# RMS norm and swish over 16384 rows: the first four stores are held back until the eleventh unit

## The chip, the cores and the metric

The kernel runs on one core of a Trainium2 chip. The metric is the device time of one execution in microseconds. Beside it there is a profiled execution, whose records give a span (from the first recorded instruction to the last), the busy time of each engine, the waits, and the packets of the DMA engines.

## The reference

The input `x` has 16 x 1024 = 16384 rows of 512 fp32 numbers. Each row is normalised and passed through swish:

```
rms = np.sqrt(np.mean(x ** 2, axis=-1, keepdims=True) + eps)
x_norm = x / rms * gamma
return (x_norm * (1.0 / (1.0 + np.exp(-x_norm)))).astype(np.float32)
```

That is 33.55 MB to read and 33.55 MB to write.

## The kernel before

**Tiles.** The 16384 rows are 128 rows for each of the 128 partitions. They are cut into eleven tiles (`sizes`, line 30) of 4, 4, 8, six times 16, 8 and 8 rows per partition. A partition's rows of one tile lie next to each other in DRAM, so a tile of n rows is moved as 128 runs of 2n KB: 8 KB for 4 rows, 16 KB for 8, 32 KB for 16.

**The ring.** One SBUF buffer, `xb`, has room for 96 rows per partition (`ring`, line 31). A row stays in its place from the load to the store: normalisation and swish are done in place. Tiles 0 to 7 are the first 96 rows and fill the ring. Tile 8 goes to the place of tiles 0, 1 and 2, and tiles 9 and 10 go to the place of tile 3. So load 8 must wait until stores 0, 1 and 2 have landed, and loads 9 and 10 until store 3 has (lines 112 to 122).

**Loads.** All loads are issued by SyncE (SP), in the order of the tiles, on its own DMA queue (q1 in the profile). The first two are placed ahead of the start-up code. Loads 0 to 7 have no wait and are issued in the first microseconds.

**Units.** Compute goes in units of four rows per partition (`cn`, line 33), so there are K = 32 units, and a tile has one, two or four of them. Unit k goes through these steps:

- `square(k)` on ScalarE (ACT): row 3 is squared and summed by one activation (line 165), rows 0 to 2 are squared into PSUM by another (line 172). The first unit of a tile waits for the tile's load.
- `sums(k)` on VectorE (DVE): a reduction of the three squared rows (line 213).
- on GpSimd (POOL): eps is added (line 147) and the power -1/2 is taken (line 154), on four numbers per partition.
- `norm(k)` on VectorE: four instructions, one for each row, that multiply by the row's factor and by gamma (line 224).
- `swish(k)` on ScalarE: one activation over the four rows (line 184).

PSUM has two buffers for the squares, so `square(k)` waits for `sums(k - 2)`. VectorE's order is sums(0), sums(1), norm(0), sums(2), norm(1), and so on.

**Stores.** Stores are issued by ScalarE on its own DMA queue (q10), in between its activations, and each waits for the swish of its tile's last unit (line 189). Their place in ScalarE's order is set by the loop at lines 201 to 208: at step k it puts down square(k), then each store whose tile ended at unit k - 2 or earlier (`ends` counts the units up to a tile's end: 1, 2, 4, 8, 12, 16, 20, 24, 28, 30, 32), then swish(k - 2). Store 0 thus comes at k = 3, store 1 at k = 4, store 2 at k = 6, store 3 at k = 10, store 4 at k = 14, and later ones at 18, 22, 26, 30, 32 and 34. At the end SyncE waits for every store that it hasn't waited for already.

Of the kernel before, what the change touches and what calls it, by code (L numbers as in the profile page):

```python
# [9 lines left out]
def kernel(  # L10
# [21 lines left out]
    early = 2  # L32
    cn = 4
    n_sq = 3
    N = sum(sizes)
    assert N * P == R, (N, R)

# [7 lines left out]
    T = len(tiles)  # L45
# [7 lines left out]
    ends = []  # L53
# [107 lines left out]
    def square(k):  # L161
        t, at, first = chunks[k]
        if first:
            nc.scalar.wait_ge(ld[t], 16)
        acc = nc.scalar.activation(  # L165
            out=junk[k % 2], in_=xb[:, at + n_sq, :], func=AF.Square,
            scale=inv_d**0.5, accum_out=ms[:, k, n_sq : n_sq + 1],
        )
        if k >= 2:
            need(acc, s_acc, k - 1)  # L170
        acc.then_inc(s_acc, 1)
        square = nc.scalar.activation(  # L172
            out=sq[k % 2][:, 0:n_sq, :], in_=xb[:, at : at + n_sq, :],
            func=AF.Square, scale=inv_d**0.5,
        )
        if k >= 2:
            need(square, s_sum, k - 1)
        square.then_inc(s_sq, 1)

    def swish(k):  # L180
        _, at, _ = chunks[k]
        rows = xb[:, at : at + cn, :]
        need(
            nc.scalar.activation(out=rows, in_=rows, func=AF.Silu), s_norm, k + 1  # L184
        ).then_inc(s_swish, 1)

    def store(t):
        need(
            nc.scalar.dma_start(out=dram(of, t), in_=buf(t)), s_swish, ends[t]
        ).then_inc(st[t], 16)  # L190
# [9 lines left out]
    stored = 0  # L200
    for k in range(K + 3):
        if k < K:
            square(k)
        while stored < T and ends[stored] <= k - 2:
            store(stored)
            stored += 1
        if 2 <= k < K + 2:
            swish(k - 2)
# [74 lines left out]
```

## Time and profile before

| | us |
|---|---|
| median of 4 runs | 160.23 (159.94 to 160.59) |
| the profiled execution, its own time | 160.33 |
| its span | 159.0 |
| VectorE busy | 139.0 (87%) |
| ScalarE busy | 125.3 (79%) |
| GpSimd busy | 91.7 (58%) |
| moved by the DMA engines | 67.15 MB, 422 GB/s on average |

In a row of a table of transfers, the share of a queue is the time that its packets took, as a part of the time of all 16 DMA engines. A row of waits reads: the engine and line that waited, whom it waited for, microseconds in total, how often, and the longest. In a timeline a row gives the start and the duration in microseconds, the engine, the line and the operation, and in brackets the idle time ahead of it and who ended it. A DMA issue is counted from the instruction's start, its landing is the moment when the last of the 16 engines reports completion.

The last four loads, and eight of the eleven stores, were issued and landed at these times (us):

| tile | rows per partition | load issued | landed |
|---|---|---|---|
| 7 | 16 | 4.4 | 81.8 |
| 8 | 16 | 62.0 | 101.2 |
| 9 | 8 | 81.3 | 115.7 |
| 10 | 8 | 81.7 | 130.2 |

| tile | store issued | landed after |
|---|---|---|
| 0 | 18.1 | 16.3 |
| 1 | 22.5 | 24.1 |
| 2 | 31.1 | 30.8 |
| 3 | 48.3 | 33.0 |
| 4 | 65.6 | 35.0 |
| 8 | 134.6 | 14.6 |
| 9 | 143.3 | 10.9 |
| 10 | 151.6 | 7.4 |

### The profile page before, as it was taken

Reading aid. Unit: us, or ns where it says so; the run is one execution under the profiler, and the core shown is the slowest. Engines: PE = TensorE matmul, PEld = TensorE weight load, DVE = VectorE, ACT = ScalarE, POOL = GpSimd, SP = SyncE. Lnnn points to the kernel's source line nnn. Section 1 sums busy time; section 2 is a strip of 40 time slices with the busy share of each in tenths; the row PEclk is TensorE's granted clock in tenths of the full one; section 3 lists DMA queues with packets and bytes.
Section 4 is the critical chain, followed back from the end, with each engine's and each line's share of the span. In section 5 each row is a group of like instructions: output and inputs, shape, how many; then the busy total and the mean of one; then the engine's idle time right before and its main releaser. Section 6 shows DMA issues by size and latency. Waiting matters only on the chain.

```text
span 159.0 us, 439 instructions
## 1 busy us (share of the span) xinstructions
DVE 139.0 (87%) x162; ACT 125.3 (79%) x129; POOL 91.7 (58%) x71
## 2 busy tenths in 40 slices
DVE  0239999999999999999999999999999999996600
ACT  0835989888888888998888888888998888883410
POOL 2035444444455555544488889888888888889000
DMA  6999999899999999999999999999999999999996
GB/s 247 422 505 412 396 433 460 371 480 418 414 398 511 396 414 441 412 429 478 412 398 478 429 412 404 429 470 425 412 437 433 412 486 412 396 495 412 400 420 284
DMA packets 3323, 67.15 MB, mean 422 GB/s; under 512 B 500, under 2 KB 500, under 8 KB 504
## 3 DMA queue, kind: packets, MB, share of 16 engines
q1 hardware_dynamic: 1584, 33.56, 49.6%
q10 hardware_dynamic: 1736, 33.57, 49.2%
q14 instruction: 3, 0.02, 0.0%
HBM read 33.56 MB, written 33.56 MB: 422 GB/s over the span
## 4 chain that ended last, share of the span: by engine, by line
DVE 84%; DMA 5%; POOL 3%; ACT 1%; issue 1%; POOLq 0%
DVE xb L224 52%; DVE ms L213 32%; DMA gamma<-in_gamma_dram 5%; POOL aeps L147 2%; ACT xb L184 1%; POOL rstd L154 1%; DVE gamma_sb L237 0%; POOL gamma L142 0%; POOL blank L141 0%; POOLq L65 0%
## 5 line engine op out<-in xcount | busy, mean ns | idle before, releaser
L224 DVE SCALAR_TENSOR_TENSOR xb<-xb,rstd,gamma_sb 128x512 f32<-128x512 f32 x128 | 87.9, 762 | 1.2 <-POOL rstd L154 1.2
L147 POOL TENSOR_SCALAR aeps<-ms 128x4 f32<-128x4 f32 x32 | 52.4, 1639 | 50.8 <-DVE ms L213 50.8
L184 ACT ACTIVATE xb<-xb 128x2048 f32<-128x2048 f32 x32 | 61.1, 1909 | 19.2 <-DVE xb L224 19.2
L213 DVE TENSOR_REDUCE ms<-sq 128x3 f32<-128x1536 f32 x32 | 56.5, 1767 | 7.0 <-ACT sq L172 7.0
L172 ACT ACTIVATE sq<-xb 128x1536 f32<-128x1536 f32 x32 | 45.9, 1434 | 0.0
L154 POOL TENSOR_TENSOR rstd<-aeps,neg_half 128x4 f32<-128x4 f32 x32 | 38.4, 1201 | 2.7
L165 ACT ACTIVATE junk<-xb 128x512 bf16<-128x512 f32 x32 | 19.7, 615 | 3.4 <-DMA xb<-in_x_dram 3.4
L165 ACT ACTIVATION_READ_ACCUMULATOR junk<-xb 128x1 f32 x32 | 6.0, 186 | 0.0
L199 ACT ACT_TABLE_LOAD x1 | 1.3, 1283 | 3.6 <-issue 3.6
L237 DVE LOAD_MASK_SELECT gamma_sb<-gamma x1 | 0.0, 14 | 2.4 <-DMA gamma<-in_gamma_dram 2.4
L141 POOL MEMSET blank<- 128x16 f32 x1 | 0.1, 111 | 1.5 <-POOLq L65 1.5
L237 DVE STREAM_SHUFFLE gamma_sb<-gamma 128x512 f32<-128x512 f32 x1 | 0.7, 718 | 0.0
L142 POOL MEMSET gamma<- 128x512 f32 x1 | 0.5, 524 | 0.0
L264 POOL MEMSET const-float32-0.0<- 128x1 f32 x1 | 0.1, 98 | 0.2 <-issue 0.2
L264 POOL MEMSET const-bfloat16-1.0<- 128x1 bf16 x1 | 0.1, 101 | 0.0
L264 POOL MEMSET const-uint8-127<- 128x1 uint8 x1 | 0.1, 101 | 0.0
L143 POOL MEMSET neg_half<- 128x4 f32 x1 | 0.1, 101 | 0.0
L264 POOL MEMSET const-float32-1.0<- 128x1 f32 x1 | 0.1, 98 | 0.0
## 6 DMA issues: line engine op xcount, KB each, us to landing
xb<-in_x_dram SPq DMA_DIRECT2D x6, 4096.0 KB, 41.6
out_dram<-xb ACTq DMA_DIRECT2D x6, 4096.0 KB, 31.2
xb<-in_x_dram SPq DMA_DIRECT2D x3, 2048.0 KB, 34.3
out_dram<-xb ACTq DMA_DIRECT2D x3, 2048.0 KB, 10.9
xb<-in_x_dram SPq DMA_DIRECT2D x2, 1024.0 KB, 5.9
out_dram<-xb ACTq DMA_DIRECT2D x2, 1024.0 KB, 20.2
scratch<-blank ACTq DMA_DIRECT2D x1, 8.0 KB, 7.8
gamma<-in_gamma_dram ACTq DMA_DIRECT2D x1, 8.0 KB
```

Source lines behind the costliest of these rows:

```text
L141: nc.gpsimd.memset(blank, 0.0).then_inc(s_blank, 1)
L142: nc.gpsimd.memset(gamma4, 0.0).then_inc(s_zero, 1)
L147: nc.gpsimd.tensor_scalar(out=aeps[:, k, :], in0=ms[:, k, :], scalar1=eps_f, scalar2=None, op0=ALU.add,),
L154: nc.gpsimd.tensor_tensor(out=rstd[:, k, :], in0=aeps[:, k, :], in1=neg_half, op=ALU.pow),
L165: acc = nc.scalar.activation(out=junk[k % 2], in_=xb[:, at + n_sq, :], func=AF.Square, scale=inv_d**0.5, accum_out=ms[:, k, n_sq : n_sq + 1],)
L172: square = nc.scalar.activation(out=sq[k % 2][:, 0:n_sq, :], in_=xb[:, at : at + n_sq, :], func=AF.Square, scale=inv_d**0.5,)
L184: nc.scalar.activation(out=rows, in_=rows, func=AF.Silu), s_norm, k + 1
L199: nc.scalar.preload_act_table_set("silu_and_others")
L213: nc.vector.tensor_reduce(out=ms[:, k, 0:n_sq], in_=sq[k % 2][:, 0:n_sq, :], op=ALU.add, axis=mybir.AxisListType.X,),
L224: ins = nc.vector.scalar_tensor_tensor(out=row, in0=row, scalar=rstd[:, k, j : j + 1], in1=gamma_sb, op0=ALU.mult, op1=ALU.mult,)
L237: nc.vector.stream_shuffle(gamma_sb, gamma4, [0] * 32), s_gld, 16
L264: nc = _bacc.Bacc("TRN2", target_bir_lowering=False, num_devices=1)
```

## The change

A number `held` is set to 11, and the loop that puts down stores does so only from step 11 on. At k = 11 stores 0, 1, 2 and 3 are due together and are put down one after the other, between square(11) and swish(9). Stores 4 to 10 are due at step 14 and later and keep their places. Nothing else is changed.

```diff
@@ -32,6 +32,7 @@
     early = 2
     cn = 4
     n_sq = 3
+    held = 11
     N = sum(sizes)
     assert N * P == R, (N, R)
 
@@ -201,7 +202,7 @@
     for k in range(K + 3):
         if k < K:
             square(k)
-        while stored < T and ends[stored] <= k - 2:
+        while k >= held and stored < T and ends[stored] <= k - 2:
             store(stored)
             stored += 1
         if 2 <= k < K + 2:
```

## The prediction

> **What bounds the kernel now.** I read the page's totals and slices first, then who waited for whom, then the chain that ended last, then the transfers by stretch, and last the stretch around the moved stores. The page (busy time by engine, busy tenths in 40 slices, transfer queues with packets, MB and share of 16 engines):
>
> ```profile
> span 159.0 us, 439 instructions
> DVE 139.0 (87%) x162; ACT 125.3 (79%) x129; POOL 91.7 (58%) x71
> ...
> DMA  6999999899999999999999999999999999999996
> ...
> q1 hardware_dynamic: 1584, 33.56, 49.6%
> q10 hardware_dynamic: 1736, 33.57, 49.2%
> ```
>
> The DMA engines are full from the first slice to the last. q1 has the loads, q10 the stores; together their packets take 98.8% of 159.0, or 157.1 us, and only 1.9 us is not packet time. At the same time VectorE (DVE) is at 9 in nearly every slice. What VectorE waits for, and then three pieces of the chain of waits (start, length):
>
> ```profile
> DVE ms L213 <- ACT sq L172: 7.0, 1, 7.0
> DVE gamma_sb L237 <- DMA gamma<-in_gamma_dram: 2.4, 1, 2.4
> DVE xb L224 <- POOL rstd L154: 1.2, 1, 1.2
> ```
>
> ```profile
> 52.35 2.65 DVE xb L224 x4
> 54.99 1.67 DVE ms L213
> ...
> 149.63 1.91 ACT xb L184
> ```
>
> VectorE waits three times in the whole execution: at the start for the first squares (7.0) and gamma (2.4), and at the end for GpSimd (1.2). Between, it repeats 2.65 + 1.67 = 4.32 us per unit. Its last row is done at 149.6, the last swish at 151.5, and the last store is issued at 151.57 and lands 7.4 us later, at 159.0. So two limits meet at the same end: the VectorE chain plus the last store, and the bytes. The store line's answer (issue ns min/median/max, first and last start, then issue to landing):
>
> ```profile
> L189 ACTq DMA_DIRECT2D out_dram<-xb x11: 338/339/339, 18.1 to 151.6; - x11
> ...
> DMA to landing us min/median/max: 7.4/24.1/35.0
> ```
>
> How close the two are: from 151.5 on the queues move 2.65 MB, of which the last store is 2.10, so 0.55 MB (1.3 us at 431 GB/s) was queued ahead of it. The engines hardly ran dry before the last store reached them.
>
> How the two queues share the engines, in 20 to 50 us and in 64 to 80 us:
>
> ```profile
> q1 hardware_dynamic: 366, 10.42, 81.8%
> q10 hardware_dynamic: 321, 2.64, 20.7%
> ```
>
> ```profile
> q10 hardware_dynamic: 114, 3.64, 52.8%
> q1 hardware_dynamic: 101, 3.24, 46.9%
> ```
>
> In the first stretch the loads are runs of 32 KB per partition and the stores mostly 8 and 16 KB, and the loads get four fifths; in the second both are 32 KB and they share evenly. The total is one (shares over 100% are packets cut by the stretch's ends).
>
> **What the Trainium skill says.** "DMA: Bandwidth & Descriptors", section "Queues, rings and completion order": an engine alternates between the queues at packet granularity. The shares just shown agree if a packet is one partition's run. The same page, "Issuing engines are not separate DMA queues": transfers from different issuers run on the same 16 engines and interleave; the trace agrees (one queue gives way to the other, the sum stays). Its section "Where 436 GB/s comes from" gives a ceiling of 435.2 GB/s, an estimate of 154.3 us for 67.15 MB at best; the trace has 157.1 us of packets. "Perfetto Trace Analysis", section "DMA Instruction — HWDGE (DVE, Sync)": the reported issue time ends when the sequencer is free for its next instruction. So the issue rows are what a burst costs ScalarE's queue.
>
> **The change part by part.** Units are numbered k. Stores 0 to 3 (4, 4, 8, 16 rows) are now issued at k = 11; before at k = 3, 4, 6, 10 (18.1, 22.5, 31.1, 48.3 us). Stores 4 to 10 are due at k = 14 and later and keep their places. No instruction is added or removed.
>
> *Where k = 11 falls.* Timeline around it:
>
> ```profile
> 52.53 0.61 ACT L165 ACTIVATE junk<-xb 128x512 bf16<-128x512 f32 x1
> ...
> 53.14 1.43 ACT L172 ACTIVATE sq<-xb 128x1536 f32<-128x1536 f32 x1
> ...
> 55.03 1.91 ACT L184 ACTIVATE xb<-xb 128x2048 f32<-128x2048 f32 x1 [0.45 <-DVE xb L224]
> ...
> 59.22 1.76 DVE L213 TENSOR_REDUCE ms<-sq 128x3 f32<-128x1536 f32 x1
> ```
>
> The first two lines are square(11). Store 3 went out at 48.34, 0.13 after square(10) began at 48.21, while that was executing; so here the first of four is issued at 52.66. Their waits are met: they need swish(7), finished before 48.3.
>
> *ScalarE's queue.* Behind the four stand swish(9), which begins at 55.03 because it waits for VectorE, then square(12), then the sum of unit 12 on VectorE at 59.22. Four issues at the 0.34 of the store row take 1.36 us and end at 54.0, hidden by square(11), which runs to 54.57, and by the 0.45 of waiting. The trace of before has no burst of stores. Its nearest rows are pairs: loads 9 and 10 on SyncE (SP) took 0.33 and 1.06, scratch and gamma on ScalarE 0.35 and 1.09, while six loads in a row took 0.33 to 0.56 each. Lower bound 1.36 us; upper 4 x 1.09 = 4.36. I take 0.34 + 3 x 0.5 = 1.8, ending at 54.5: cost nothing. Without this cover each microsecond would pass to swish(9); square(12) ends at 58.88 today, 0.34 ahead of its reader, and VectorE never catches up what it loses.
>
> *SyncE's queue.* Load 8 (rows 96 to 111) waits for stores 0 to 2, loads 9 and 10 for store 3. In bytes at 0.431 MB/us:
> - To 52.7 us the queues moved 21.90 MB in before; now all of it is loads, of 25.17 MB for 96 rows. 3.27 MB are left. With 1.5 us for a store's first bytes (the first load took 1.0), they meet stores at 54.2 with 2.6 MB to go; at four to one that is 3.3 MB, 7.7 us: load 7 is in at about 62, against 81.8 before (issued 4.39, 77.4 to landing).
> - Stores 0 to 2 are 4.19 MB, of which 0.66 have gone; 3.53 MB alone take 8.2 us: landed at about 71.5 (before 61.9). Load 8 is issued at 71.6, 9.6 us later than today, first bytes at 73.
> - By then 1.2 MB of store 3 are gone. The other 3.0 share evenly with load 8: 14 us, landed at 88.5 (before 81.3), when loads 9 and 10 are issued. Load 8 has 1.2 MB left, shared with store 4 (issued 65.6): in at 94 (before 101.2). Loads 9 and 10 (16 KB runs against 32 KB stores, one third) take 2.1 x 3 / 0.431 = 14.6 us each: in at about 108.5 and 123 (before 115.7 and 130.2).
> - Needed, at 4.316 us a unit from square(11) at 52.53: load 8 at square(24), 108.6; load 9 at square(28), 125.9; load 10 at square(30), 134.5. Margins of 14, 17 and 11 us, against 7, 10 and 4 before. Cost nothing.
>
> *Does an engine run dry?* To 62 there are loads. After that store 3 and store 4 (10 us each alone) follow without a gap. When the last load ends near 122, 51.8 MB have moved, 18.2 of it stores; 25.2 MB have been issued by 117.4. The 7 MB left last 16 us, to 138, and store 8 is issued at 134.6. From there queue and dates are those of before, since the same bytes have moved.
>
> *One queue alone.* Loads are alone for about 36 us more, stores for about 20 more. In 5 to 15 us the load queue alone shows 438 GB/s (101.9%), in 144 to 151 the store queue alone 440 (102.3%), against 436 and 431 shared. Stretches this short are uncertain by a packet at each end, some per cent. I take no difference and keep 1% either way: 55 us x 1% = 0.55 us.
>
> *Sum.* VectorE 0, burst 0, late loads 0, queues 0 to 0.1: span 159.1. The profiled execution was 160.33, 1.33 around its span, and 0.10 over the median of 160.23. So 159.1 + 1.33 - 0.10 = 160.3 us.
>
> **Rivals.**
> *The burst stalls VectorE (slower).* Place: swish(9) behind the four issues. If the last three cost 1.06 each, they end at 52.66 + 3.52 = 56.18, 1.15 late; less 0.34 of slack VectorE loses 0.81. At 4.36 us it loses 1.65. It decides from a burst of 2.71 us (52.66 to 55.37), and up to 1.3 us can vanish in the bytes queued ahead of the last store. Unhidden: 161.0, at worst 161.9. For it: two pairs with 1.06 and 1.09. Against: six loads in a row without one.
> *A queue alone leaves gaps (slower).* At 1%: 160.8. For: nothing alternates to cover a hand-over. Against: the slices of 9 before the first store.
> *Unmixed transfers are quicker, or GpSimd's last wait shrinks (faster).* The bytes could end up to 1.3 us earlier before the last store is late for its own sake: 158.9 at best; 1% gives 159.7. The 1.2 us that VectorE waits for GpSimd at the end, if gone, leaves the bytes where they are. Against: packets fill 157.1 of 159.0.
> *The change does only part of what it says.* 3.27 of the 25.17 MB still load beside stores; this moves no end: 160.3.
>
> **How the numbers follow.** About 0.3% (0.5 us) is what a measurement can tell from no change. The forecast has 0.78; the burst 0.08, gaps 0.07, a late load or dry queue that I missed 0.02; quicker transfers 0.05. So slower 0.17, same 0.78, faster 0.05. The forecast's own spread is 159.9 to 160.7 from the runs of before (159.94 to 160.59); widened to the 1% cases and to the unhidden 0.81 us: 159.7 to 161.0.
>
> **What would show it.** Right: VectorE still at 2.65 and 1.67 with three waits; four store issues between 52.6 and 55, with swish(9) at 55.0; SyncE waiting for stores to about 71.5 and 88.5; q10 empty before 54; the last store issued near 151.6. Wrong: a wait of VectorE for L172 or L165 in mid-run, ScalarE waiting for a load after 100 us, or slices under 9 in the DMA row near 54, 62 or 72 us.

## The result: 0.45% slower, and the profile after

The changed kernel took 160.93 us in the median of 39 runs (160.35 to 162.13), the kernel before 160.16 us in 60 runs beside it. The ratio is 1.0045, 95% interval 1.0032 to 1.0058: slower by some 0.7 us. A later series of six runs (`r1` below) gave 1.0078 (1.0059 to 1.0098); the two intervals don't meet, so two series of one kernel can differ by 0.3%, and smaller differences between ratios of different series can't be read. Ratios leave out executions more than 1.5% above the fastest of the same kernel, which in `r7` are 5 of 22 (165.56 to 167.58 us). The forecast was 160.3 us and no change. The time lies in the range given, but the likeliest case was not the one that came.

The profiled execution of the changed kernel took 160.93 us, with a span of 159.6. Its page, as before (busy time, busy tenths in 40 slices, queues with packets, MB and share of 16 engines):

```profile
span 159.6 us, 439 instructions
DVE 138.8 (87%) x162; ACT 125.2 (78%) x129; POOL 65.4 (41%) x71
...
DMA  7999999999999899999999999999999999999995
...
q1 hardware_dynamic: 1584, 33.56, 49.8%
q10 hardware_dynamic: 1736, 33.57, 49.0%
```

Same packets, same bytes, and still no idle stretch to speak of. But a share is a share of the span, so each is multiplied by it: the stores' packets (q10) took 0.490 x 159.6 = 78.2 us of 16 engines, as before (0.492 x 159.0 = 78.2); the loads' packets (q1) took 0.498 x 159.6 = 79.5 us against 0.496 x 159.0 = 78.9. The span grew by 0.6 us, and so did the time of the load packets. (A share is printed to a tenth of a per cent, 0.16 us; the packet records below are finer.)

What VectorE waits for, and the two ScalarE activations and the burst around k = 11 (timeline: start, length):

```profile
DVE ms L214 <- ACT sq L173: 7.0, 1, 7.0
DVE gamma_sb L238 <- DMA gamma<-in_gamma_dram: 2.2, 1, 2.2
```

```profile
50.51 1.91 ACT L185 ACTIVATE xb<-xb 128x2048 f32<-128x2048 f32 x1 [0.45 <-DVE xb L225]
50.52 1.83 ACTq L190 DMA_DIRECT2D out_dram<-xb  x4
...
54.83 1.91 ACT L185 ACTIVATE xb<-xb 128x2048 f32<-128x2048 f32 x1 [0.45 <-DVE xb L225]
```

The burst of four took 1.83 us and cost ScalarE nothing: swish(9) at 54.83 still waits the same 0.45 us for VectorE. VectorE has no wait in mid-run, and the wait for GpSimd at the end is gone, so the last store is issued early:

```profile
L190 ACTq DMA_DIRECT2D out_dram<-xb x11: 338/339/488, 50.5 to 150.0; - x11
...
DMA to landing us min/median/max: 9.5/20.7/38.9
```

At 150.0 instead of 151.6, and yet it lands at 159.6 instead of 159.0: 9.5 us after its issue instead of 7.4. Compute is done sooner and the bytes later. The waits of SyncE for stores came out as worked out (load 8 issued at 72.2, loads 9 and 10 at 87.9; forecast 71.6 and 88.5):

```profile
SPq L121 <- DMA out_dram<-xb: 67.2, 1, 67.2
SPq L123 <- DMA out_dram<-xb: 15.4, 1, 15.4
```

Where the transfers fell behind is seen by what had begun to move by a given time. Before, to 52 us, to 64 us and to 90 us:

```profile
DMA packets 1416, 21.73 MB, mean 418 GB/s; under 512 B 276, under 2 KB 276, under 8 KB 280
```

```profile
DMA packets 1642, 26.77 MB, mean 418 GB/s; under 512 B 308, under 2 KB 308, under 8 KB 312
```

```profile
DMA packets 2021, 38.12 MB, mean 424 GB/s; under 512 B 340, under 2 KB 340, under 8 KB 344
```

After, to the same times:

```profile
DMA packets 1192, 22.01 MB, mean 423 GB/s; under 512 B 260, under 2 KB 260, under 8 KB 264
```

```profile
DMA packets 1498, 26.65 MB, mean 416 GB/s; under 512 B 291, under 2 KB 291, under 8 KB 295
```

```profile
DMA packets 2011, 37.79 MB, mean 420 GB/s; under 512 B 340, under 2 KB 340, under 8 KB 344
```

With loads alone the changed kernel is ahead by 0.28 MB at 52 us. At 64, when the stores have met the last loads, it is 0.12 MB behind, and at 90, when load 8 has met store 3, 0.33 MB. At 431 GB/s the last is 0.77 us. But these rows count a whole packet where it begins. If each packet is counted by the part of it that has passed, the changed kernel is 0.20 MB ahead at 52 us, level at 64 and 0.19 MB behind at 90, which is 0.44 us.

The packet records show more. A packet of 32, 16 or 8 KB takes 1.213, 0.611 or 0.309 us nearly always, alone or beside the other queue, read or write. Some take longer, loads most of all (they have 0.88 of the 1.05 us named next). I add up what is over these three values, divide by 16 engines, and call it the **excess**. After the first 5 us it is 0.76 us in before and 1.05 us in the change. In the change 0.35 of it falls in 60.3 to 61.5 us (15 packets, the last of load 7) and 0.40 between 75 and 87 us (0.30 on loads, 0.10 on stores). Before has 0.16 at 21.3 us, 0.12 at 45.7 us, 0.06 at 60.5 us.

A second part comes on top. The end is set by the slowest of the 16 engines. In before the last store's sixteen completions arrive at 158.30 us on average and the last at 158.97; in the change at 158.60 and 159.57. So half of the 0.6 us is in the mean, and the other half in how far the slowest engine is behind it.

### The profile page after: what moved, and what is told of

Its sections match the earlier page's. It is cut to its first block, busy times and chain, and to the rows that moved or that the text cites. A ratio compares the mean times of both kernels' runs of the same rounds, so it can differ in the third digit from the quotient of the medians.

```text
span 159.6 us, 439 instructions
## 1 busy us (share of the span) xinstructions
DVE 138.8 (87%) x162; ACT 125.2 (78%) x129; POOL 65.4 (41%) x71
## 4 chain that ended last, share of the span: by engine, by line
DVE 85%; DMA 5%; ACT 1%; issue 1%; POOL 0%; POOLq 0%
DVE xb L225 53%; DVE ms L214 31%; DMA gamma<-in_gamma_dram 5%; ACT xb L185 1%; DVE gamma_sb L238 0%; POOL gamma L143 0%; POOL blank L142 0%; POOLq L66 0%
## 5 line engine op out<-in xcount | busy, mean ns | idle before, releaser
L148 POOL TENSOR_SCALAR aeps<-ms 128x4 f32<-128x4 f32 x32 | 20.6, 644 | 75.1 <-DVE ms L214 75.1
L155 POOL TENSOR_TENSOR rstd<-aeps,neg_half 128x4 f32<-128x4 f32 x32 | 44.0, 1376 | 2.7
```

Source lines behind the costliest of these rows:

```text
L148: nc.gpsimd.tensor_scalar(out=aeps[:, k, :], in0=ms[:, k, :], scalar1=eps_f, scalar2=None, op0=ALU.add,),
L155: nc.gpsimd.tensor_tensor(out=rstd[:, k, :], in0=aeps[:, k, :], in1=neg_half, op=ALU.pow),
```

## The experiments

Each changes only the steps at which stores are put down, unless it says otherwise. Ratios are to the kernel before, run on the same chip beside it. A trace shows one execution, which needn't be near its kernel's median: that of `r8` is the fastest of its 22, those of `r4` and `r11` are the slowest of their 9.

**The two kernels again.** `r1` is the changed kernel unaltered, `r2` the kernel before.

> The changed kernel once more, for a second profile and a closer time. Transfer theory (packets take longer where four stores at once meet the last loads, and again where load 8 starts beside store 3): ratio to before 1.003 to 1.006; by 48 us about 0.2 MB more has moved than in before, and that lead is lost between 56 and 90 us; VectorE without a wait in mid-run. Chance theory (the slow packets fall elsewhere in each execution and the order of the transfers has no part in it): the lead and the loss are not at these places again. Burst theory (the four issues stall VectorE): a wait of VectorE for L173 near 55 us, which the first profile does not show.

> The kernel before once more, for a second profile. Transfer theory: the packets' time again near 157.1 us for a span near 159.0, and no long loss between 56 and 90 us. Chance theory: a span anywhere between 158.7 and 160 with slow packets at other places than in the first profile.

Measured: `r1` 161.6 us, ratio 1.0078 (1.0059 to 1.0098), span of the profiled execution 160.3; `r2` 160.14 us with a span of 158.8. The lead is there again (by parts of packets, `r1` is 0.28 MB ahead of `r2` at 52 us), and so are two places: load packets longer by 0.34 us at 60.0 to 60.8 and by 0.16 at 52.7 to 54.7. Store packets are longer by 0.11 at 75 to 76.5, as in the first trace (0.10). But load packets between 76 and 87 us, longer by 0.30 in the first trace, are so by only 0.10 here, and at 90 us `r1` is only 0.05 MB behind `r2`. The second profile of before has its excess at 20 to 21 (0.16), 44 to 46 (0.32) and 60 us (0.10), so near the places of the first. The chance theory falls for the lead and for 60 us; for 76 to 87 us this pair doesn't exclude it. What makes `r1` late is above all its slowest engine: the mean completion of the last store is 158.50 us, the last 160.27. The burst theory falls too, as VectorE again has no wait in mid-run. Its wait for GpSimd at the end was missing in the second profile of before as well (last store issued at 150.5), so that wait comes and goes by itself.

**held = 7 and held = 10.**

```diff
-    held = 11
+    held = 7
```

> held = 7: stores 0, 1 and 2 together at k = 7 (about 35 us), store 3 at k = 10 as before. The burst falls amid the loads and not at their end. Transfer theory (end of the loads matters): ratio to before 0.998 to 1.002. If any burst of stores costs, wherever it falls: 1.002 to 1.005. If only the later store 2 and load 8 cost: load 8 is issued at 62 us or somewhat later, ratio about 1.000.

> held = 10: stores 0 to 2 join store 3 at k = 10, where before has store 3 already, one unit (4.3 us) earlier than in the change. Transfer theory: most of the loss, since the burst still meets the last loads, ratio 1.002 to 1.005. If the loss came from running dry near 62 us it should be smaller by far, under 1.001, since the stores then come 4.3 us earlier.

Measured: held = 7 160.41 us, ratio 1.0009 (0.9992 to 1.0026); held = 10 161.08 us, 1.0046 (1.0027 to 1.0064). With held = 7 the burst meets the loads from 35.8 us on and its load packets are 0.35 us longer until 41 us; next to nothing is lost at 59 to 62 (0.02), and the total excess is 0.61 us. With held = 10 it is 1.25 us: 0.36 at 47.7 to 49.6, 0.23 at 61.4 to 62.1, and 0.53 at 83.5 to 84.5, on 15 packets, as the last packets of store 3 give way to the first of store 4. One unit earlier didn't help, so running dry near 62 us is not the cause. A burst as such needn't show in the time.

**held = 14, so that the engines do run dry.**

```diff
-    held = 11
+    held = 14
```

> held = 14: stores 0 to 4 together at k = 14 (about 63 us), after the loads of 96 rows are in (about 61 us for loads alone). If the bytes set the end, the transfer engines stand idle for about 2 to 4 us and all of it shows at the end: ratio 1.015 to 1.03. If the VectorE chain sets the end, which in the change has 1.5 us in hand, most of it is hidden: under 1.010.

Measured: 166.31 us, 1.0374 (1.0313 to 1.0435), above both expectations. The profile's slices, VectorE and transfers:

```profile
DVE  0249999999999999999999999999999999990000
...
DMA  7999989999899953999799989999998999999996
```

The 5 and the 3 are the slices from 57.7 to 65.9 us: the last load packet ends at 61.2, and the first store, issued at 63.6, has its first packet at 64.5. VectorE is full as ever and done 14 us before the end (last store issued at 150.2). In moved bytes it is 0.4 us ahead of before at 56 us, 3.2 us behind at 64 and 5.1 at 88, with 1.07 us of longer packets at 78 to 81 (0.99 of it on store packets), when load 8, issued at 75.1, has its first packets (79.9). The span is 5.7 us longer than that of before. The bytes set the end, and what they lose is not given back.

**Which store, and which size.** The loop is put as a table of steps:

```diff
-        while stored < T and ends[stored] <= k - 2:
-            store(stored)
+        while stored < T and max(due.get(stored, 0), ends[stored] + 2) <= k:
+            store(order[stored])
```

`r6`: due = {2: 11, 3: 11}. `r7`: due = {3: 13}. Both in the tiles' order. `r8`: due = 11 for stores 0 to 3, in the order 3, 0, 1, 2; the `order` in the lines above is in `r8` alone.

> Stores 0 and 1 at their places of before (k = 3 and 4), stores 2 and 3 together at k = 11. The last loads meet 16 KB and 32 KB runs instead of a row of 8 KB runs, and load 8 is still issued some 8 us later than in before. Theory that the row of small stores at the end of the loads is the cause: ratio 1.000 to 1.002. Theory that late stores at the end of the loads cost whatever their size, or that the later load 8 costs: 1.003 to 1.006.

> Stores 0 to 2 at their places of before, store 3 alone at k = 13 (about 59 us), so that loads 9 and 10 start later. The store queue is empty for some us before it, while loads are still going. Small-store theory and load-8 theory: 0.998 to 1.002. Theory that it is store 3's lateness: 1.003 or more.

> As the change, but in the burst at k = 11 store 3 (32 KB runs) goes first and stores 0, 1, 2 after it. The last loads then share evenly with large runs, and load 8 is issued about 10 us later than in the change (near 82 us, landed near 102, needed at 108). Small-store theory: ratio 1.000 to 1.002. Load-8 theory: as the change or more, 1.004 to 1.008.

Measured: `r6` 160.54 us, 1.0017 (1.0001 to 1.0032); `r7` 160.92 us, 1.0048 (1.0029 to 1.0067); `r8` 161.24 us, 1.0059 (1.0046 to 1.0072). `r6` came out as the theory of the small stores said (1.000 to 1.002), but that theory falls with `r7` and `r8`. The others don't fit all three either: late stores or a late load 8 should have cost 1.003 to 1.006 in `r6`, and a late load 8 nothing in `r7`. In the trace of `r8` its 32 KB runs meet the loads with 0.82 us of longer load packets between 52.6 and 55.7 us, more than the 8 KB runs of the change at that place (0.09), and then little more (0.10). This trace has a span of 159.1, as before, so it doesn't show what the median loses (1.0 us). `r6` loses 0.61 us at 52.8 to 55.4, where its stores begin anew, and 0.09 after. So in the traces the longer packets move to where the streams meet. `r7` doesn't fit a sum of longer packets: its excess (0.92 us) and the mean completion of its last store (158.41 us) are like those of before, but the last engine completes at 159.87, 1.46 us after the mean. What is slower there are a few engines at the end.

**The transfers alone.** All compute is removed, and stores wait for loads in its place. `r9` has the table below; `r10` has 6 for each of the four. In both, store 4 waits for load 6 too, so in `r10` it goes right behind the burst (at 53.1 us, against 65.4 in the change):

```diff
-        need(
-            nc.scalar.dma_start(out=dram(of, t), in_=buf(t)), s_swish, ends[t]
-        ).then_inc(st[t], 16)
...
+    after = {0: 3, 1: 3, 2: 4, 3: 5}
+    for t in range(T):
+        nc.scalar.wait_ge(ld[t], 16)
+        need(
+            nc.scalar.dma_start(out=dram(of, t), in_=buf(t)),
+            ld[after.get(t, min(t + 2, T - 1))], 16,
+        ).then_inc(st[t], 16)
```

> Loads and stores alone: squares, sums, normalisation and swish are left out, and the rows are stored as they were loaded. Same tiles, ring, queues and ring waits; stores begin about when those of before do (stores 0 and 1 after load 3, 2 after load 4, 3 after load 5, later ones after the load two further on). If the transfers alone set the end, as both theories of the transfers say: span near 157.5 to 158.5, ratio to before 0.990 to 0.999. It is the base for the next run.

> The same without compute, but stores 0 to 3 all wait for load 6 (about 51 us), as in the change. Theory that the order of the transfers costs by itself (packets take longer each time that a stream starts or changes its run length beside the other): 0.003 to 0.006 over the run before this one. Theory that it needs the engines too (their instruction fetches, which take a transfer engine, or their waits): no more than 0.001 over it.

Measured: mixed 159.76 us, ratio 0.997 (0.9959 to 0.9982); held 160.46 us, 1.0018 (1.0001 to 1.0035). Held is 0.70 us over mixed, and the ratios differ by 0.0048: as much as the change costs (0.0045), without one squared row. The pages of the two, mixed first:

```profile
span 158.4 us, 79 instructions
...
q1 hardware_dynamic: 1584, 33.56, 49.8%
q10 hardware_dynamic: 1728, 33.56, 49.2%
```

```profile
span 159.4 us, 79 instructions
...
q1 hardware_dynamic: 1584, 33.56, 50.0%
q10 hardware_dynamic: 1728, 33.56, 49.0%
```

Load packets took 0.498 x 158.4 = 78.9 us and 0.500 x 159.4 = 79.7 us, store packets 77.9 and 78.1. The excess after 5 us is 0.61 and 1.33 us. Mixed has it at 25, 31 and 57 us (0.14, 0.13, 0.28); held has 0.59 at 60.1 to 60.6, on the last 16 packets of load 7, and 0.54 at 83.7 to 85.6, on load packets. (The records don't name the engine, but packets can be joined end to start. Joined so, these lie between an engine's last packet of store 3 and its first of store 4, on nearly every engine, and so do those of 83.5 to 86 us in the change and in held = 10.) To 52 us held had begun 22.03 MB against 21.77, to 90 us 37.76 against 38.05: the lead of the full kernels and a loss like that of the first pair. No engine fetched instructions in these two (the queue of instructions is absent from their pages), so the theory that it needs the compute engines falls as the main cause.

Three pairs of traces side by side (us; the last two columns are of the sixteen completions of the last store):

| | span | excess | mean completion | last after the mean |
|---|---|---|---|---|
| before, first and second | 159.0, 158.8 | 0.76, 0.89 | 158.30, 158.47 | 0.67, 0.31 |
| the change, first and second | 159.6, 160.3 | 1.05, 1.00 | 158.60, 158.50 | 0.97, 1.77 |
| transfers alone, mixed and held | 158.4, 159.4 | 0.61, 1.33 | 158.13, 158.82 | 0.28, 0.52 |

In these six traces, and in the six others whose transfers have all bytes and no pause (all but `r5` and `r12`), the mean completion is 157.5 us plus the excess, to about 0.1 us. So longer packets account for the mean. From mixed to held they are most of the loss, 0.69 of 0.93 us. In the whole kernels the mean has less: it is later by 0.30 of 0.60 us from the first trace of before to the first of the change, and by 0.03 of 1.49 between the second ones. The rest is the lateness of the slowest engine, which no run here explains.

**Load 8 later.** The held transfers with one more wait:

```diff
+        if t == 8:
+            waits = waits + [3]
         for u in waits:
```

> Without compute and with stores 0 to 3 held, as the run before it in this document, but load 8 waits for store 3 too, so that no load is in flight between the end of load 7 (about 63 us) and the landing of store 3 (about 81 us). Of the two places where that run lost time, 60 us (0.59 us of longer packets) stays and the one near 84 to 86 us (0.54 us) should go, if it is load 8's packets beside the end of store 3 that cost: 0.3% under that run, near 0.9985 to 0.9995 of before. If the restart of the load stream costs wherever it falls: the loss only moves to about 83 us, and the time stays at 1.001 to 1.003 of before.

Measured: 160.88 us, 1.0040 (1.0019 to 1.0060). The loss at 60 us stays (0.42). Load 8 is now issued at 81.0, when store 3 has landed, and the longer load packets at 83.7 to 85.6 are gone, as no load is in flight until 84.9. In their place six store packets at 84.7 to 85.2 are up to 1.23 us longer (0.29 us in all), just as load 8's first packets begin. The 0.10 us on store packets in the change, at 75.4 to 76.2, stands at the same point: load 8's first packet there is at 76.3. Two engines end 1.6 and 1.7 us after the mean. Taking load 8 away from the end of store 3 saved no time; the trace has less excess than held (1.14 us), but later engines.

**Fewer bytes.** The changed kernel without store 5:

```diff
-            store(stored)
+            if stored != 5:
+                store(stored)
```

> The changed kernel without store 5: 16 rows per partition (4.19 MB, 9.7 us of transfer time) of the output are left out, all compute stays. If the bytes set the end of the changed kernel, the end falls back to the VectorE chain plus the last store, which is issued at 150.0 to 151.6 us and then needs about 6.3 us: span 156.3 to 157.9, ratio to before 0.983 to 0.993. If the VectorE chain or a late load set it, the time stays near 1.004.

Measured: 159.14 us, 0.9931 (0.9914 to 0.9948). Its slices, and its stores:

```profile
DMA  6999999999999998999999999999999960999947
```

```profile
L190 ACTq DMA_DIRECT2D out_dram<-xb x10: 338/338/500, 50.6 to 151.4; - x10
...
DMA to landing us min/median/max: 6.3/15.2/39.1
```

The engines pause from about 129 to 135 us, so whatever was lost at 60 and 85 is caught up, and the last store finds an empty queue: 6.3 us from issue to landing, at 157.8. This is the end of the VectorE chain with the last store, at the upper edge of what was expected. With that one store more the changed kernel ends 1.8 us later, though its last store is issued 1.4 us sooner (150.0).

## Why the prediction was right and wrong

**Right.** Two limits near each other at the end, with the bytes the one that can't be bought off: VectorE was done 1.5 us sooner in the profile after, without effect, and the rival that GpSimd's last wait might shrink and "leaves the bytes where they are" came true. The burst of four issues: 1.83 us against 1.8 worked out, hidden. SyncE's queue: load 7 in at 64.2 (62), store 2 at 72.1 (71.5), store 3 at 87.9 (88.5), load 8 at 97.3 (94), loads 9 and 10 at 111.9 and 126.4 (108.5 and 123). No load came late. Some of this was luck: a transfer's first bytes were put 1.5 us after its issue, from the 1.0 us of the first load, which had idle engines. Beside a running stream it was 3.4 us for store 0 (50.52 to 53.90) and 4.1 for load 8 (72.17 to 76.29). That the burst went 2.1 us sooner than forecast made up for the first. Load 8's first bytes came 3.3 us later than worked out (76.3, not 73), and so did its landing, within its margin. The trace of before had it: store 0, issued at 18.13, has its first packet at 21.65. The engines don't run dry; `r5` shows what it costs if they do.

**Wrong.** The step that failed is "From there queue and dates are those of before, since the same bytes have moved", with the term that carried it, queues "0 to 0.1". It took a packet's time to depend on its size alone. That holds in the long stretches, loads alone, stores alone, or mixed in one steady pattern. It doesn't always hold where a stream starts, stops or meets the other anew. There packets took 0.1 to 0.8 us longer on an average engine within a few microseconds. The change has fewer such microseconds in its first half, and gains 0.20 MB by 52 us (0.28 with packets counted where they begin), and dearer ones at 60 and, in the first trace, at 75 to 87 us. The term was 0.7 us by the transfers alone (160.46 against 159.76). In the traces of the whole kernels longer packets are only part of the loss, as the table shows, and the lateness of the slowest engine is the rest.

The rival nearest in time, "a queue alone leaves gaps" at 160.8, had its sign by the wrong mechanism: alone, each queue ran at its best (loads 4 and 5 in the changed kernel at 1.213 us a packet, end to end). Its 55 us x 1% happened to be as large as what was lost elsewhere.

The place of the burst was off as well. I put it at 52.66, after the start of square(11), because store 3 had gone out just after the start of square(10). It went at 50.52, with the start of swish(8): in before, store 3 had been waiting for swish(7), done at 48.3, and not for its turn. Only the dates above hung on it.

**Open.** Which meetings cost, and why. Shown is that order alone does it (`r9`, `r10`), that the price sits in a few clusters of longer packets and in late engines, and that clusters move with the stream that starts (`r6`, `r8`, `r11`). Not explained is why held = 7, whose load stream also stops at 69 and has its next packet at 75.4 us, pays only 0.10 us from 72 to 88, nor why one or two engines end 1.3 to 1.8 us after the mean in some executions (`r1`, `r4`, `r6`, `r7`, `r11`). A packet that follows an instruction fetch of 8 KB took up to 1.85 us in the change and 1.75 in before, instead of 1.21; `r11` has late engines without fetches, so they are not needed for it. The order also sets which addresses are read and written at one time; no run separates the two.

## What to carry to other kernels

Where packets fill 98.8% of the span, the order of the transfers is not free even if no byte is added and no engine waits: a place where loads and stores meet anew can cost some tenths of a microsecond, and it is not given back unless the transfers pause later (`r12`). Compare what has moved by a few fixed times in the two traces, not only the end. And an unbroken mixture of two streams was no worse here than the two in turn, so there was nothing to win by parting them.

## What the runs showed of the hardware that I had not expected

- A transfer issued on an empty queue beside a running stream has its first packet 3.4 to 4.8 us after the start of its issue (23 times in these traces). With idle engines it is 0.84 us for stores (`r5`, `r12`) and 1.0 for the first load.
- ScalarE's queue runs ahead of its arithmetic: four stores placed after square(11) were issued from 50.52 us on, 1.8 us before square(11) began at 52.33.
- Issues in a row on ScalarE took 0.34, 0.44, 0.44 and 0.49 us; the pair of loads that took 0.33 and 1.06 in before took 0.33 and 0.48 in the change.
- One and the same GpSimd addition takes 0.66 us or 2.65 us. In before it switches at 78 us and stays; in the change it never does (mean 644 ns against 1639). It is not the change that decides: `r2` doesn't switch, `r4` and `r12` do. VectorE feels it only at the end, by 1.2 us.
